# Retention keys and outputs turned in 32x32 blocks by VectorE, and put in place by DMAs, in a Griffin-style encoder block

## The chip, the cores and the metric

The kernel runs on one core of a Trainium2 chip. The metric is device time in microseconds of one execution, the median of several runs; lower is better. A core has a matrix engine (TensorE, PE in the rows, with its weight loads as PEld), VectorE (DVE), ScalarE (ACT), GpSimd (POOL) and SyncE (SP), which here only issues DMAs. Each engine works off its own list of instructions in order. A DMA is issued by an engine's queue and lands later. All matrix inputs and all results are float32.

## The reference, cut to what matters

One layer on 512 tokens of width 2048: a combined projection of the normalised input, a sparse attention (mixer A), a retention (mixer B), two gated merges, an output projection and a gated embedding. The part that the change touches is mixer B, with 8 heads of key and value width 128, and the gate behind it:

```python
rq = rope(rq.reshape(B, L, R_HEADS, R_KEY_DIM), positions)
rk = rope(rk.reshape(B, L, R_HEADS, R_KEY_DIM), positions) * (R_KEY_DIM ** -0.5)
...
scores = jnp.einsum('bnqhd,bnkhd->bnhqk', qc, kc) * intra_decay
intra = jnp.einsum('bnhqk,bnkhe->bnqhe', scores, vc)
kv = jnp.einsum('bnkhd,bnkhe->nbhde', kc * to_end[:, :, None], vc)
...
y = (intra + cross).reshape(B, L, R_HEADS, R_VAL_DIM)
mu = jnp.mean(y, axis=-1, keepdims=True)
var = jnp.mean((y - mu) ** 2, axis=-1, keepdims=True)
y = ((y - mu) * lax.rsqrt(var + EPS)).reshape(B, L, R_WIDTH) * gn_gain
...
b_out = retention_mixer(rq, rk, rv, ret_gn_gain) * jax.nn.silu(rz)
```

The sum over keys for `kv` needs the keys with tokens on the partitions, while the projection gives them with the key's channels on the partitions. The normalised output `y` has tokens on the partitions, and the gate and the next projection want channels there. Both have to be turned once per head.

## The kernel before, in words

The large products are done in float32 accuracy from two-part splits: a weight tile `wraw` (128x1024) is loaded by SP, ScalarE rounds it to `wh` (L156), VectorE subtracts to get `wl` (L161) and, for some tiles, adds two raw tiles in place (L163, tile `wraw`). `gemm_pair` makes two 128-column blocks of the projection together, with seven half-sized products; it issues 112 matmuls (L326) of 512 or 256 columns. Its results leave PSUM through ScalarE copies (`pv`, `e1`, `e2`, `e3`, L265, shown as `pv` and `e`) and VectorE sums (`e_t`, L269), and are added up into the tile `go` (L1094).

The order of the work is written out by hand. `step()` advances a counter, the tick; `gemm_pair` calls it after every second matmul, so that a pair lasts 56 ticks. `later(n, f)` puts `f` off by n ticks. Each engine's instructions stand in the order in which these calls come, and no scheduler changes it: an instruction that waits holds up all that stand behind it on its engine, and a DMA issue that waits holds up SP. Weight loads for coming units (L132) stand on SP between the other DMAs; for some tiles POOL issues an adding DMA on top (L119).

The retention of a head h runs in the shadow of these pairs. For each of the 8 heads there is one pair that projects query and key, and then two pairs for the merge gates. When the key has come out of the first (the second call of `rotate`, its tick is called 0 here), a list `steps` (L993 to L996) sets the rest off:

- tick 3, 5, 7: the rotary sums on VectorE (L904 to L906); tick 9: `queries`, tile `qt` (L913)
- tick 24: `scores` on PE (L920), and `keys(0)`: three PE transposes of 128x128 into the PSUM tile `ps_t` (L931, in `turn`); tick 28: `decay`, tile `at` (L924)
- tick 29: `keys(1)`: ScalarE copies `ps_t` to `kn` with a factor per partition (L939)
- tick 39, 41, 43: `states`: PE makes `ps_kv` from `kn` and the values `rvh` (L945), ScalarE and VectorE chain the states
- tick 51: `values_out` on PE, tile `ps_y` (L960, L962); tick 57: `norm`, with a POOL power (L972); tick 70: `scale`, tile `yn` (L979)
- tick 90: `back(0)`: four PE transposes of `yn` into `ps_t`; tick 94: `back(1)`: ScalarE copies them to `yT` with the group norm's gain (L988), and two ticks later SP stores `yT` to the DRAM tensor `yd` (L989)

So a head has 7 PE transposes, and the 8 heads have 56. After the 8 heads, four pairs make the gate `rz`; in them SP loads `yd` back as `y` (L1127), POOL multiplies it into the gate (L1122) and stores to `bd` (L1123). Much later `b_load` (L1261) loads `bd`, and `split` (L850, L851) makes its two parts for the projection `project_b`.

PSUM has 8 banks that all tiles share; `U` tiles are 69 slots of 128x512 float32.

Of the kernel before, what the change touches and what calls it, by code (L numbers as in the profile page):

```python
# [9 lines left out]
F32 = mybir.dt.float32  # L10
# [4 lines left out]
AF = mybir.ActivationFunctionType  # L15
OP = mybir.AluOpType

L = 512
D = 2048
KT = D // 128  # L20
NH = 8
NT = L // 128
# [13 lines left out]
def block_kernel(tc, xT, pT, posb, posq, w_in, w_v, w_r0, w_r1, w_ik, w_a, w_b, w_o, w_ple, w_gate,  # L36
                 w_gt, w_pt, fgb, tab, gains, cst, dec, out, out_a, out_b):
    nc = tc.nc
    pe, dve, act, pool, sp = nc.tensor, nc.vector, nc.scalar, nc.gpsimd, nc.sync

    with contextlib.ExitStack() as ctx:
# [10 lines left out]
        def U(name, dt=F32):  # L52
            return up.tile([128, L], dt, name=name, tag="u")
# [4 lines left out]
        def P(name):  # L58
            return pp.tile([128, L], F32, name=name, tag="p")
# [4 lines left out]
        def tok(t):  # L64
            return slice(128 * t, 128 * t + 128)
# [114 lines left out]
        def later(n, f):  # L180
            if n <= 0:
                return f()
            tick[1] += 1
            heapq.heappush(soon, (tick[0] + n, tick[1], f))
# [260 lines left out]
        ng, fg, gn = g_sb[:, 0:16], g_sb[:, 16:32], g_sb[:, 32:40]  # L445
# [397 lines left out]
                       for i in range(4 * len(b[1]))])  # L843
            bg.append(lambda run=run: waiting.append(run))

        def split(src, name, lag=0):

            h = U(name + "h", F32R)
            l = U(name + "l", F32R)
            later(lag, lambda: act.activation(h, src, AF.Copy))  # L850
            later(lag and lag + 1, lambda: dve.tensor_sub(l, src, h.bitcast(F32)))  # L851
            return h, l

        def three(o, lhs, rhs, cl, cr):
# [29 lines left out]

        yd, bd, zd, qd, kd = (dp.tile([NH, 128, L], F32, name=n) for n in ("yd", "bd", "zd", "qd", "kd"))
        vd = dp.tile([2, 7, 128, L], F32, name="vd")

        def retention(h):

# [34 lines left out]
                dve.tensor_mul(at.rearrange("p (t q) -> p t q", t=NT), E["ps"].rearrange("p (t q) -> p t q", t=NT),  # L924
                               dect[:, None, 0:128].to_broadcast([128, NT, 128]))

            def turn(src, n):

                ps = P("ps_t")
                for t in range(n):  # L930
                    pe.transpose(ps[:, tok(t)], src[:, tok(t)], ident)  # L931
                return ps[:, 0:128 * n]

            def keys(i):
                if i == 0:
                    E["pk"] = turn(E[1], 3)
                else:
                    E["kn"] = U("kn")
                    act.activation(E["kn"][:, 0:384], E["pk"], AF.Copy, scale=dect[:, 256:257])  # L939

            def states(i):
                if i == 0:
                    ps = E["ps"] = P("ps_kv")
                    for t in range(3):
                        pe.matmul(ps[:, tok(t)], E["kn"][:, tok(t)], rv[:, tok(t)], start=True, stop=True)  # L945
                elif i == 1:
                    E["s"] = U("state")
                    act.activation(E["s"][:, 0:128], E["ps"][:, 0:128], AF.Copy)
                else:
                    for t in (1, 2):  # L950
                        dve.scalar_tensor_tensor(E["s"][:, tok(t)], E["s"][:, tok(t - 1)], g128, E["ps"][:, tok(t)],
                                                 op0=OP.mult, op1=OP.add)

            def values_out(t):
                if t == 0:
                    E["py"] = P("ps_y")
                    E["st"] = S("gst", 24)
                    E["mv"] = S("gmv", 8)
                o = E["py"][:, tok(t)]
                pe.matmul(o, E["at"][:, tok(t)], rv[:, tok(t)], start=True, stop=(t == 0))  # L960
                if t:
                    pe.matmul(o, E["qt"][:, tok(t - 1)], E["s"][:, tok(t - 1)], start=False, stop=True)  # L962
# [19 lines left out]

            def back(i):
                if i == 0:
                    E["pt"] = turn(E["yn"], NT)
                else:
                    E["yT"] = U("yT")
                    act.activation(E["yT"], E["pt"], AF.Copy, scale=gn[:, h:h + 1])  # L988
                    later(2, lambda: sp.dma_start(yd[h], E["yT"]))  # L989

            steps = [(9, queries), (24, scores), (24, lambda: keys(0)), (28, decay), (29, lambda: keys(1))]
            steps += [(n, lambda i=i: states(i)) for i, n in enumerate((39, 41, 43))]
            steps += [(51, lambda t=t: values_out(t)) for t in range(NT)]  # L993
            steps += [(57, norm), (70, scale), (90, lambda: back(0)), (94, lambda: back(1))]
            return rotate

        x_wanted = collections.deque(x_away)
# [119 lines left out]
        for n, u in enumerate(u_rz):  # L1117
            y = B("y2")

            def b_out(i, o, y=y, n=n):  # L1120
                act.activation(o, o, AF.Silu)
                pool.tensor_mul(o, o, y[:, L * i:L * i + L])  # L1122
                pool.dma_start(out=bd[2 * n + i], in_=o)  # L1123

            def y_load(y=y, n=n):
                for i in range(2):
                    sp.dma_start(y[:, L * i:L * i + L], yd[2 * n + i])  # L1127

            later(16 if n else 0, y_load)
            gate_pair(u, b_out)  # L1130
# [128 lines left out]
        def b_load(h):  # L1259
            t = U("bk")  # L1260
            sp.dma_start(t, bd[h])  # L1261
            later(25, lambda: bparts.append(split(t, "b", 1)))

        for n in range(NH // 2):
            if n == NH // 2 - 1:
# [461 lines left out]
```

## Time and profile before

| | |
|---|---|
| median of 3 runs | 1656.47 us (1655.72 to 1656.68) |
| the profiled execution | 1655.59 us |
| its span, first to last instruction | 1653.8 us |
| PE busy | 1645.1 us, 99% of the span |
| DVE, ACT, POOL busy | 79%, 58%, 14% |
| granted TensorE clock, mean | 0.999 of full speed |
| DMA moved | 362.69 MB, 219 GB/s over the span |

The span is the part of the execution that the trace covers; 1.8 us of the profiled execution lie around it. Matmuls are pipelined: a matmul's row shows how long it was under way, and the distance between the starts of two matmuls shows what one costs. In a timeline, equal neighbours are merged into one row with a count.

### The profile page before, as it was taken

How to read it: one execution, taken by the hardware profiler on the slowest of the kernel's cores; microseconds unless marked ns; L12 is line 12 of the kernel's file. 1: busy time of each engine (PE TensorE's matmuls, PEld its weight loads, DVE VectorE, ACT ScalarE, POOL GpSimd, SP SyncE). 2: the span in 40 equal slices, each digit the busy share in tenths (PEclk: the TensorE clock that was granted, in tenths of full speed). 3: DMA queues.
4: the chain of work that ended last, by engine and by line, in shares of the span. 5: the costliest groups of instructions: out<-in, count | busy, mean ns of one | idle time of the engine just before them, and what ended most of it. 6: DMA issues, size and time to landing. Idle time of an engine off the chain costs nothing.

```text
span 1653.8 us, 25255 instructions
## 1 busy us (share of the span) xinstructions
PE 1645.1 (99%) x9334; PEld 1448.0 (88%) x9334; DVE 1305.6 (79%) x2022; ACT 966.2 (58%) x1489; POOL 231.8 (14%) x257
## 2 busy tenths in 40 slices
PE   9999999999999999999999999999999999999998
PEld 8988888888888888888888888888888888888997
DVE  8788879888888888877766766787768877888884
ACT  7556545555555555767776766566644444576653
POOL 2100111111111111112331122100000111100112
PEclk9999999999999999999999999999999999999999
DMA  8327999788788788788988888997565788765973
GB/s 311 117 88 240 326 258 275 192 205 221 187 210 217 188 208 222 188 210 247 255 231 229 213 234 220 247 375 278 178 209 179 189 217 219 211 218 145 247 229 141
DMA packets 129531, 362.69 MB, mean 219 GB/s; under 512 B 15552, under 2 KB 24256, under 8 KB 129408
## 3 DMA queue, kind: packets, MB, share of 16 engines
q1 hardware_dynamic: 89152, 239.77, 41.5%
q0 software_dynamic: 27440, 98.32, 31.7%
q10 hardware_dynamic: 12816, 23.00, 3.8%
q8 instruction: 73, 1.20, 0.3%
q14 instruction: 50, 0.41, 0.1%
HBM read 313.32 MB, written 47.71 MB: 218 GB/s over the span
## 4 chain that ended last, share of the span: by engine, by line
PE 96%; DVE 2%; ACT 1%; issue 0%; DVEq 0%; ACTq 0%
PE ps_p L326 26%; PE ps_v L326 17%; PE ps_q L326 9%; PE ps_r L326 9%; PE ps_w L233 3%; PE ps_w L232 3%; PE ps_w L234 3%; PE ps_vn L874 2%; PE ps_vn L873 2%; PE ps_vn L872 2%; PE ps_iq L232 1%; PE ps_iq L234 1%; PE ps_iq L233 1%; PE ps_pg L233 1%; PE ps_pg L232 1%; PE ps_pg L234 1%
## 5 line engine op out<-in xcount | busy, mean ns | idle before, releaser
L161 DVE TENSOR_TENSOR wl<-wraw,wh 128x1024 fp32r<-128x1024 f32 (+3 forms) x472 | 568.4, 1216 | 157.7 <-ACT wh L156 155.3
L156 ACT ACTIVATE wh<-wraw 128x1024 fp32r<-128x1024 f32 (+3 forms) x471 | 486.8, 1041 | 240.6 <-DVE wraw L163 118.9
L119 POOL DMA_DIRECT2D wraw<-w_in x120 | 106.3, 960 | 574.7 <-DVE wl L161 386.6
L326 PE MATMUL ps_p<-hs,wh 128*128 128x512 f32 x640 | 160.8, 393 | 0.0
L265 ACT ACTIVATE e<-ps_p 128x512 f32<-128x512 f32 x152 | 90.4, 594 | 119.3 <-PE ps_p L326 117.1
L326 PEld LDWEIGHTS ps_p<-hs,wh 128*128 128x128 f32 x640 | 115.0, 189 | 20.5
L326 PE MATMUL ps_p<-hs,wl 128*128 128x256 f32 x640 | 91.8, 284 | 0.0
L326 PEld LDWEIGHTS ps_p<-hs,wl 128*128 128x128 f32 x640 | 83.1, 192 | 0.0
L326 PE MATMUL ps_q<-ha,wh 128*128 128x512 f32 x320 | 80.7, 394 | 0.0
L326 PE MATMUL ps_v<-ha,wh 128*128 128x512 f32 x320 | 80.0, 392 | 0.0
L326 PE MATMUL ps_v<-hs,wh 128*128 128x512 f32 x320 | 79.0, 389 | 0.0
L326 PE MATMUL ps_p<-ha,wh 128*128 128x512 f32 x320 | 79.0, 389 | 0.0
L326 PE MATMUL ps_r<-hs,wh 128*128 128x512 f32 x320 | 79.0, 389 | 0.0
L800 ACT ACTIVATE mk<-relf,thr 128x512 f16<-128x512 f32 (+3 forms) x128 | 66.7, 555 | 16.5 <-DVE go L1094 12.0
L1094 DVE TENSOR_TENSOR go<-e_t 128x256 f32<-128x256 f32 x160 | 68.2, 426 | 5.7
L326 PEld LDWEIGHTS ps_v<-hs,wh 128*128 128x128 f32 x320 | 60.1, 188 | 12.5
L326 PEld LDWEIGHTS ps_p<-ha,wh 128*128 128x128 f32 x320 | 60.1, 188 | 12.5
L326 PEld LDWEIGHTS ps_r<-hs,wh 128*128 128x128 f32 x320 | 60.1, 188 | 12.5
L269 DVE TENSOR_TENSOR e_t<-ps_p,pv 128x512 f32<-128x512 f32 x48 | 33.1, 690 | 47.6 <-ACT e L265 47.5
L326 PEld LDWEIGHTS ps_v<-ha,wh 128*128 128x128 f32 x320 | 59.5, 188 | 12.1
L119 POOL DMA_DIRECT2D wraw<-w_o x24 | 21.1, 938 | 348.6 <-DVE t L356 191.4
L326 PEld LDWEIGHTS ps_q<-ha,wh 128*128 128x128 f32 x320 | 57.5, 189 | 12.1 <-issue 1.7
(481 smaller groups left out, 3812.3 us busy)
## 6 DMA issues: line engine op xcount, KB each, us to landing
wraw<-w_in SPq DMA_DIRECT2D x170, 512.0 KB, 5.1
wraw<-w_in POOLq DMA_DIRECT2D x120, 512.0 KB, 8.3
wraw<-w_o SPq DMA_DIRECT2D x32, 512.0 KB, 4.9
wraw<-w_o POOLq DMA_DIRECT2D x24, 512.0 KB, 6.9
wraw<-w_gate SPq DMA_DIRECT2D x24, 512.0 KB, 5.1
wraw<-w_v SPq DMA_DIRECT2D x16, 512.0 KB, 9.0
wraw<-w_b SPq DMA_DIRECT2D x16, 512.0 KB, 5.8
wraw<-w_a SPq DMA_DIRECT2D x16, 512.0 KB, 3.8
```

What stands on the lines that cost most here:

```text
L119: pool.dma_start(out=view(raw_tiles[r], nk, cols), in_=src[:, k0:k0 + nk, :], accum_op=OP.add)
L156: act.activation(h, raw, AF.Copy)
L161: dve.tensor_sub(l, raw, h.bitcast(F32))
L232: pe.matmul(o, h[:, k, w], a, start=(s == order[0]), stop=False)
L233: pe.matmul(o, h[:, k, w], b, start=False, stop=False)
L234: pe.matmul(o, l[:, k, w], a, start=False, stop=(s == order[-1]))
L265: act.activation(E[n], src, AF.Copy)
L269: f(t, x, y)
L326: pe.matmul(o[:, co], w[:, k], src, start=(n < 4 and begin and k == 0 and j == 0), stop=(ended[n] == 16), skip_group_check=True)
L800: act.activation(bias_e[b][i // per][:, ln * (i % per):ln * (i % per + 1)], relf[:, :ln], AF.Sign, bias=thr[:, q:q + 1])
L872: pe.matmul(o, a[:, tok(t)], h[:, k], start=(s == 0), stop=False)
L1094: dve.tensor_add(o[:, q], c0, c1)
```

## The change

Both turns leave TensorE. VectorE transposes each 32x32 block in place of the 128x128 turn and writes the blocks in an order by which four DMAs, one for each group of 32 partitions, can put them in DRAM as the turned matrix with its columns in a known order of blocks.

For the keys: `keys(0)` at tick 11 is the VectorE transpose into `kb`; `keys(1)` at tick 21 issues four stores from SP to a new DRAM tensor `krd` (32 partitions each, 128 pieces of 384 bytes); `keys(2)` at tick 29 issues one load of `krd` into `kr` (192 KB); `keys(3)` at tick 36 is the ScalarE copy to `kn`, now from `kr`, which puts the blocks in order and applies the factor. `states`, `values_out` and `norm` come two ticks later than before, `scale` stays.

For the outputs: `back(0)` at tick 74 is the VectorE transpose into `yb`; `back(1)` at tick 84 issues four stores to `yd` (128 pieces of 512 bytes each). The copy `yT` is gone. The order of blocks in `yd` is undone by POOL's multiplication, and the gain moves into `split` of the loaded `bd`.

```diff
+        def split(src, name, lag=0, gain=None):
...
+            def low():
+                if gain is None:
+                    dve.tensor_sub(l, src, h.bitcast(F32))
+                else:
+                    dve.scalar_tensor_tensor(l, src, gain, h.bitcast(F32), op0=OP.mult, op1=OP.subtract)
+
+            later(lag, lambda: act.activation(h, src, AF.Copy, scale=1.0 if gain is None else gain))
+            later(lag and lag + 1, low)
...
+        krd = dp.tile([NH, 128, 384], F32, name="krd")
...
-            def turn(src, n):
-                ps = P("ps_t")
-                for t in range(n):
-                    pe.transpose(ps[:, tok(t)], src[:, tok(t)], ident)
-                return ps[:, 0:128 * n]
+            def turn(src, n, name):
+                b = U(name)
+                w = 32 * n
+                dve.transpose(out=b[:, 0:4 * w].rearrange("p (j t c) -> p t j c", j=4, t=n),
+                              in_=src[:, 0:4 * w].rearrange("p (t j c) -> p t j c", t=n, j=4))
+                return b[:, 0:4 * w]
+
+            def send(b, dst):
+                w = b.shape[1] // 4
+                for i in range(4):
+                    sp.dma_start(dst.rearrange("(j r) (i x) -> i r j x", j=4, i=4)[i],
+                                 b[32 * i:32 * i + 32, :].rearrange("r (j x) -> r j x", j=4))
 
             def keys(i):
                 if i == 0:
-                    E["pk"] = turn(E[1], 3)
+                    E["kb"] = turn(E[1], 3, "kb")
+                elif i == 1:
+                    send(E["kb"], krd[h])
+                elif i == 2:
+                    E["kr"] = U("kr")
+                    sp.dma_start(E["kr"][:, 0:384], krd[h])
                 else:
                     E["kn"] = U("kn")
-                    act.activation(E["kn"][:, 0:384], E["pk"], AF.Copy, scale=dect[:, 256:257])
+                    act.activation(E["kn"][:, 0:384].rearrange("p (t i c) -> p i t c", t=3, i=4),
+                                   E["kr"][:, 0:384].rearrange("p (i t c) -> p i t c", i=4, t=3),
+                                   AF.Copy, scale=dect[:, 256:257])
...
             def back(i):
                 if i == 0:
-                    E["pt"] = turn(E["yn"], NT)
+                    E["yb"] = turn(E["yn"], NT, "yb")
                 else:
-                    E["yT"] = U("yT")
-                    act.activation(E["yT"], E["pt"], AF.Copy, scale=gn[:, h:h + 1])
-                    later(2, lambda: sp.dma_start(yd[h], E["yT"]))
-
-            steps = [(9, queries), (24, scores), (24, lambda: keys(0)), (28, decay), (29, lambda: keys(1))]
-            steps += [(n, lambda i=i: states(i)) for i, n in enumerate((39, 41, 43))]
-            steps += [(51, lambda t=t: values_out(t)) for t in range(NT)]
-            steps += [(57, norm), (70, scale), (90, lambda: back(0)), (94, lambda: back(1))]
+                    send(E["yb"], yd[h])
+
+            steps = [(9, queries), (11, lambda: keys(0)), (21, lambda: keys(1)), (29, lambda: keys(2))]
+            steps += [(24, scores), (28, decay), (36, lambda: keys(3))]
+            steps += [(n, lambda i=i: states(i)) for i, n in enumerate((41, 43, 45))]
+            steps += [(53, lambda t=t: values_out(t)) for t in range(NT)]
+            steps += [(59, norm), (70, scale), (74, lambda: back(0)), (84, lambda: back(1))]
...
-                pool.tensor_mul(o, o, y[:, L * i:L * i + L])
+                ov = o.rearrange("p (t i c) -> p t i c", t=4, i=4)
+                v = y[:, L * i:L * i + L].rearrange("p (i t c) -> p t i c", i=4, t=4)
+                pool.tensor_mul(ov, ov, v)
...
-            later(25, lambda: bparts.append(split(t, "b", 1)))
+            later(25, lambda: bparts.append(split(t, "b", 1, gn[:, h:h + 1])))
```

## Rows read from the trace of the kernel before

**Rows 1.** The page: busy time, share of the span and instructions of each engine.

```profile
PE 1645.1 (99%) x9334; PEld 1448.0 (88%) x9334; DVE 1305.6 (79%) x2022; ACT 966.2 (58%) x1489; POOL 231.8 (14%) x257
```

**Rows 2.** Waits of PE, whole span: total us, times, longest.

```profile
PE ps_warm L487 <- DVE warm L464: 1.0, 1, 1.0
```

**Rows 3.** Stretches: us, busy of PE, PEld, DVE, ACT, POOL, clock, DMA share, GB/s.

```profile
256.00:790.00 534.00, 534.00 (x3182) 474.10 (x3181) 448.26 (x691) 309.27 (x407) 90.37 (x96) 1.00 0.81 213
292.30:299.10 6.80, 6.80 (x52) 6.41 (x50) 6.73 (x9) 2.92 (x4) 0.00 (x0) 1.00 0.44 158
```

**Rows 4.** Instructions on tile ps_t: ns min/median/max, first and last start.

```profile
L931 PE MATMUL ps_t<-cs,yn x32: 270/272/273, 318.1 to 754.8; 128*128 128x128 f32 x32
L931 PE MATMUL ps_t<-cs,go x24: 272/273/273, 293.7 to 730.2; 128*128 128x128 f32 x24
```

**Rows 5.** Timeline of PE, head 0: start us, us, instruction, count.

```profile
293.67 0.49 PE L931 MATMUL ps_t<-cs,go 128*128 128x128 f32 x3
293.91 0.95 PE L326 MATMUL ps_q<-ha,wl 128*128 128x256 f32 x6
294.71 1.12 PE L326 MATMUL ps_r<-hs,wl 128*128 128x256 f32 x8
295.66 0.52 PE L326 MATMUL ps_p<-hs,wl 128*128 128x256 f32 x3
...
298.46 0.83 PE L945 MATMUL ps_kv<-rvh,kn 128*128 128x128 f32 x6
299.05 2.10 PE L326 MATMUL ps_v<-ha,wh 128*128 128x512 f32 x8
300.99 1.11 PE L326 MATMUL ps_v<-ha,wl 128*128 128x256 f32 x8
```

**Rows 6.** Timeline of DVE, head 0.

```profile
291.78 0.55 DVE L913 TENSOR_TENSOR qt<-go,dect 128x384 f32<-128x384 f32 x1
292.25 2.35 DVE L161 TENSOR_TENSOR wl<-wraw,wh 128x1024 fp32r<-128x1024 f32 x2
294.64 1.23 DVE L163 TENSOR_TENSOR wraw<-wraw 128x1024 f32<-128x1024 f32 x1
```

**Rows 7.** Timeline of ACT, head 0; in brackets idle time before and what ended it.

```profile
295.98 1.06 ACT L156 ACTIVATE wh<-wraw 128x1024 fp32r<-128x1024 f32 x1 [4.28 <-DVE wraw L163]
```

**Rows 8.** Timeline of SP's queue, head 0, and the landing times of yd<-yT.

```profile
293.49 0.33 SPq L132 DMA_DIRECT2D wraw<-w_in  x1
...
320.33 0.33 SPq L989 DMA_DIRECT2D yd<-yT  x1
320.70 1.46 SPq L132 DMA_DIRECT2D wraw<-w_in  x3
...
DMA to landing us min/median/max: 2.0/2.1/2.2
```

**Rows 9.** Issues by line: KB each, median us to landing.

```profile
y<-yd SPq DMA_DIRECT2D x8, 256.0 KB, 6.2
```

**Rows 10.** Stores in pieces of 128 and 64 bytes (rd<-rvx), and their landing.

```profile
L614 SPq DMA_DIRECT2D rd<-rvx x2: 382/440/499, 73.0 to 73.4; - x2
...
DMA to landing us min/median/max: 1.8/1.8/1.9
```

**Rows 11.** Timelines of DVE and PE, head 6.

```profile
666.94 2.35 DVE L161 TENSOR_TENSOR wl<-wraw,wh 128x1024 fp32r<-128x1024 f32 x2
...
669.62 1.12 PE L326 MATMUL ps_p<-hs,wl 128*128 128x256 f32 x8
...
672.42 0.83 PE L945 MATMUL ps_kv<-rvh,kn 128*128 128x128 f32 x6
```

**Rows 12.** Timelines of DVE and PE, head 3.

```profile
478.11 1.22 DVE L161 TENSOR_TENSOR wl<-wraw,wh 128x1024 fp32r<-128x1024 f32 x1
...
485.44 0.83 PE L945 MATMUL ps_kv<-rvh,kn 128*128 128x128 f32 x6
```

**Rows 13.** Instructions of line L1122, columns as in rows 4.

```profile
L1122 POOL TENSOR_TENSOR go<-go,y x8: 1292/1512/1898, 783.8 to 848.2; 128x512 f32<-128x512 f32 x8
```

More of the change, by code (lines that the diff above doesn't have):

```diff
@@ L844, in block_kernel @@
             bg.append(lambda run=run: waiting.append(run))
-        def split(src, name, lag=0):
+        def split(src, name, lag=0, gain=None):
             h = U(name + "h", F32R)
             l = U(name + "l", F32R)
-            later(lag, lambda: act.activation(h, src, AF.Copy))
-            later(lag and lag + 1, lambda: dve.tensor_sub(l, src, h.bitcast(F32)))
+            def low():
[5 more added lines that the diff above has]
+            later(lag and lag + 1, low)
             return h, l
```

## The prediction

> **What bounds the kernel now.** I read the page first: PE is busy 99% of the span [rows 1]. That alone says little, since a pipelined matmul's row is longer than what the matmul costs, so the waits come second. PE waited once, for 1.0 us, before the first matmul [rows 2]; from then on no semaphore held it up. Third, the retention stage by itself (256 to 790 us): PE is busy all of its 534 us at full clock, VectorE 448 us (84%), ScalarE 309 us (58%), and the DMA engines 81% [rows 3]. So the time there is the sum of what PE issues, every other engine has been early enough so far, and two things decide: how much PE issue the change takes out, and whether any of what it puts in makes PE wait for the first time.
>
> **What is removed.** There are 32 + 24 transposes of 272 ns each [rows 4]; 56 x 0.272 = 15.2 us would be the wrong sum, because a matmul starts before its forerunner has ended. The cost is the distance between starts. From 293.67 to 294.71 PE starts three transposes and six 256-column matmuls; the eight 256-column matmuls after them take 0.95 us to the next start, 0.119 each [rows 5]. So 1.04 - 6 x 0.119 = 0.33 us for three transposes, 0.109 each. The output turn's transposes have the same shape and duration [rows 4], so 56 x 0.109 = 6.1 us. That is all the change can gain: PE does not wait for PSUM banks, so the two banks that a head no longer needs are worth nothing, and neither is the ScalarE copy `yT`.
>
> The Trainium skill (VectorE: DVE Perf Modes, The three transpose paths) gives a 128x128 TensorE transpose as 390 ns in bf16 and VectorE's block transpose as 311 ns. By that figure the estimate would be 56 x 0.39 = 21.8 us; the spacing of the starts says otherwise, and the measurement decides.
>
> **What is added for the keys.** I follow head 0, in the times of the trace of before.
> - VectorE's transpose of 128x384 follows `qt`, of the same size, which took 0.55 us and held the engine 0.47 (291.78 to 292.25) [rows 6]. No row has a transpose; between 0.2 (half of it) and 0.94 (double) I take 0.47, the nearest row's. The result is there at 292.8.
> - SP issues four stores. Two issues in a row start 0.37 apart, and a store of 256 KB landed after 2.0 to 2.2 us [rows 8]. Issues at 292.85 to 293.96, last landing at 296.1. The weight load at tick 23, at 293.49 before [rows 8], now stands behind them, 0.8 us later. Nobody needs its data soon: SP is eight weight tiles ahead of use. Late next would be POOL's adding DMA and the rounding of that tile; if that cover were gone it would be 0.8 us a head.
> - SP then holds the load of `kr` until the stores have landed, to 296.1, and the next weight loads stand behind it by some tenths, under the same cover. No row shows such a load in this place. Below stands the 2.0 us of a store [rows 8], above the 6.2 us of the loads of `yd` [rows 9]. I take 2.4, near the lower end, because the DMA engines are busy 44% in this stretch against 81% in the stage [rows 3], with one weight load in front. `kr` is there at 298.5.
> - ScalarE: the rounding at 295.98 waits for VectorE's addition [rows 6, 7], so it starts 0.47 later, at 296.45; it and the next one keep ScalarE until 298.5. The copy to `kn`, about 0.55 by `qt`'s size, ends at 299.1, 6.85 us after VectorE's hand-over at 292.25.
> - PE: `ps_kv` started at 298.46. Three transposes less bring it 0.33 forward; two ticks more are four 512-column matmuls at 1.94 / 8 = 0.24 each, 0.97 back [rows 5]. PE comes there at 299.1 too: a wait of 0 to 0.1 us. The two ticks by which the state chain and `values_out` move shift demand and supply alike.
>
> Head 6 is the tightest. Its hand-over is at 666.94 and `ps_kv` starts 5.48 us later; in head 0 that is 6.21, in head 3 7.33 [rows 5, 6, 11, 12]. The second `wl` of head 6 ends at 666.94 + 2.35 = 669.29, and PE reads it at 669.62 [rows 11]. With VectorE 0.47 later and PE 0.33 earlier, PE waits 0.5 there, and then `kn` (673.8) is 0.25 later than PE (673.55): 0.75 in all. In head 3 there are 1.1 us to spare. Taking five heads like head 0, two like head 3 and head 6: 5 x 0.1 + 0.75 = 1.3 us given back.
>
> **What is added for the outputs.** `yn` is ready before tick 74, and nothing on PE waits for `yb`: the gate stage reads `yd` for its first heads after the eighth. SP stands at the four stores until VectorE has turned `yn`; before, it stood until ScalarE had made `yT`, and later (the store went at 320.33 [rows 8]). Three issues more are 3 x 0.37 = 1.1 us of SP, hidden by the same lead of the weight loads. VectorE gets 0.61 us more (0.47 x 512/384) in front of the next weight splits. VectorE had 86 of 534 us idle [rows 3] and the change takes 8 x (0.47 + 0.61) = 8.6 of them, so on average there is room. Locally I bound the effect by nothing and 0.5 us a head (head 6's case) and take 0.1: 0.8 us.
>
> **What costs nothing.** POOL's product (1.5 us, eight times [rows 13]) now reads runs of 32; if it took double, 1.5 us would stand before the next adding DMA of POOL, which the lead of the weight loads hides. The split with gain keeps its count of instructions, and the matmuls of the last pairs and of the projection hide it. DRAM traffic grows by 8 x 2 x 192 KB = 3 MB of 363 MB.
>
> **The sum.** 6.1 - 1.3 - 0.8 = 4.0 us. The profiled execution took 1655.59 us, so 1651.6; the median of the runs is 0.9 us above that execution, so **1652.5 us**. A measurement of this kernel tells about 0.2%, 3.3 us, from no change: below 1653.2 is faster, above 1659.8 slower. The forecast's own range is 1650.4 (no wait at all) to 1653.1.
>
> **The rivals.**
>
> *The round trip eats the gain.* If the transpose holds VectorE twice as long (0.94), or `kr` lands half a microsecond later, five heads wait about 0.55 us and head 6 1.2, with 0.8 for the outputs 4.8 us: 1655.2 us, no change that can be told. For it: head 0's margin came out at zero, from a load whose time no row gives. Against: I added each step in series and took the longer of two ScalarE roundings as certain.
>
> *The load of `kr` lands late, and PE waits in every head.* The place is `states` in front of PE, in order, so each delay past the margin goes straight to the end. At the 6.2 us of the loads of `yd` [rows 9] the copy comes 3.8 us later: 5 x 3.85 + 4.55 + 2 x 2.7 = 29 us of waits, +24 net, 1680 us. At 4.3 us it is 14 us, +8.7 net, 1665 us. It decides from a landing of about 3.6 us, where the net loss passes 3.3 us. For it: 81% DMA load in the stage; against: the quiet stretch just here [rows 3], and 192 KB in place of 256.
>
> *The short pieces make the stores slow.* If stores in pieces of 384 bytes landed after twice the 2.1 us, `kn` would come 2.1 us later, with 5 x 2.15 + 2.85 + 2 x 1.0 = 15.6 us of waits: 1666 us. Stores in pieces of 128 and 64 bytes landed after 1.8 to 1.9 us [rows 10], which speaks against it, though at a quiet time. The Trainium skill (DMA: Bandwidth & Descriptors, Specifications) states 512 bytes as the least transfer for full rate and a read-modify-write below it; by that rule this rival would be the outcome, and the 64-byte stores of this trace do not bear it out for single small stores.
>
> *It does not do what it says*, in that PE's issue goes on at the same pace for another reason: transposes that lay in the shadow of weight loads would free nothing. The spacing of the starts [rows 5] shows each taking its own 0.109 us, so I give this almost nothing.
>
> **How the numbers follow.** The forecast 0.50 (faster); the round trip that eats the gain 0.32 (same); late `kr` 0.13 and slow stores 0.05 (slower). The range goes from 1650.0 (the whole 6.1 us, and half a microsecond of scatter) up into the late-`kr` case at 1661.0; what is left out is most of the two slower cases and a little below.
>
> **What would show it.** In the profile of after, the PE rows of `ps_t` are gone and PE has fewer instructions. If the forecast holds, the waits of PE name `ps_kv` for ScalarE's `kn` with some tenths of a microsecond, in few heads, head 6 first. VectorE's transposes show 0.5 to 0.7 us, the stores land after about 2 us, and `kr` after 2.4. A `kr` landing near 4 us and eight PE waits at `ps_kv` of over 1 us each would show the slower case; waits of PE at an L326 matmul for `wl` would show VectorE's room as the mis-sized term. A gain clearly over 6.1 us would mean that the spacing of starts misses a part of what a transpose costs.

## The result, and the profile after

The changed kernel takes 1665.43 us (median of 6 runs, 1662.95 to 1669.14) against 1656.19 us before (6 runs, 1655.72 to 1656.68): ratio 1.006, 95% interval 1.0046 to 1.0074. It is slower by 9.2 us. The prediction said 1652.5, so the sign was wrong, and the time lies above the range. The profiled execution of after took 1665.03 us, 9.44 more than that of before.

The page of after, its span, its lines of busy time and the chain's shares by engine:

```profile
span 1663.2 us, 25259 instructions
...
PE 1643.0 (99%) x9278; PEld 1442.4 (87%) x9278; DVE 1313.7 (79%) x2038; ACT 963.3 (58%) x1481; POOL 233.0 (14%) x257
...
PE 87%; DVE 6%; ACT 3%; DMA 3%; issue 1%; SPq 0%; DVEq 0%; ACTq 0%
```

PE has lost its 56 transposes and still shows 99%, as in [rows 1], because the rows of pipelined matmuls overlap. The busy share would have told nothing; the chain does, since the parts that are not PE have grown to 13%. The waits of PE (engine, tile and line <- what ended it: us in all, times, longest) answer to [rows 2]:

```profile
PE ps_kv L969 <- ACT kn L961: 11.2, 7, 2.6
PE ps_warm L487 <- DVE warm L464: 1.0, 1, 1.0
PE ps_r L326 <- DVE wl L161: 0.2, 1, 0.2
```

In seven of eight heads PE now stands in front of `ps_kv` for the copy `kn`. That copy waits for the load `kr`. The instructions of the new tiles (columns as in [rows 4]; under each queue's line its time from issue to landing):

```profile
L940 DVE STREAM_TRANSPOSE kb<-go x8: 569/572/575, 293.1 to 736.6; 128x384 f32<-128x384 f32 x8
L948 SPq DMA_DIRECT2D krd<-kb x32: 303/423/1032, 293.7 to 738.8; - x32
DMA to landing us min/median/max: 1.6/1.7/2.5
...
L958 SPq DMA_DIRECT2D kr<-krd x8: 338/338/338, 297.6 to 741.4; - x8
L961 ACT ACTIVATE kn<-kr,dect x8: 614/614/617, 300.8 to 744.6; 128x384 f32<-128x384 f32 x8
DMA to landing us min/median/max: 3.0/4.0/5.0
```

The transpose, the stores and the copy are near what was forecast; the load is not: 4.0 us at the median, not 2.4. Head 4 shows the whole round trip. Its chain of waits (start us, us, engine or DMA and what):

```profile
544.83 0.55 DVE qt L921
545.38 0.50 DVE kb L940
...
547.21 1.68 DMA krd<-kb
549.04 4.44 DMA kr<-krd
553.56 0.62 ACT kn L961
554.23 0.94 PE ps_kv L969 x6
```

The DMAs of SP's queue in the same head say why the load is long:

```profile
545.89 1.75 SPq L948 DMA_DIRECT2D krd<-kb  x4
547.74 0.38 SPq L132 DMA_DIRECT2D wraw<-w_in  x1
549.04 0.34 SPq L958 DMA_DIRECT2D kr<-krd  x1
549.47 0.38 SPq L132 DMA_DIRECT2D wraw<-w_in  x1
```

The 512 KB weight load of tick 23 goes out at 547.74, between the stores (tick 21) and the read-back (tick 29). It landed 5.2 us after its issue, at 552.98; `kr`, issued 1.3 us behind it, came in at 553.48, half a microsecond after it. So the small load that PE waits for shared the DMA engines with a large one that nobody awaited.

Where the time went, stretch by stretch, I take from the starts of PE's matmuls. In each trace and head I read the start of the first matmul at or after a tick, counted from the second `rotate`; the lengths between two such starts, after minus before, are summed over the eight heads. The variants of the experiments stand here too (us):

```
ticks of a head          12-26  26-38  38-47  47-58  88-100 100-112 | stage
the changed kernel       -2.57  +0.91 +13.15  +0.16   -3.36   +0.17 | +8.45
kr_first                 -2.58  +2.04  +2.06  +0.16   -3.36   +0.17 | -1.51
kr_from_act              -2.58  +1.61 +26.68  +0.82   -3.36   +0.17 | +23.34
kr_from_act_one_load     -2.57  +0.92 +10.53  +0.16   -3.36   +0.16 | +5.85
keys_only                -2.57  +0.91 +15.54  +0.15   +0.11    0    | +14.13
outputs_only              0      0      0      0      -3.36   +0.17 | -3.19
queries_behind           -1.91  +0.33  +1.57  +0.16   -3.36   +0.16 | -3.05

                         12-26  26-38  38-72         88-100 100-112 | stage
states_later             -2.57  +0.91  +1.2          -3.36   +0.05  | -3.76
first_and_later          -2.57  +1.21  +1.2          -3.36   +0.07  | -3.46
queries_behind_later     -2.57  +0.27  +0.45         -3.36   +0.06  | -5.15
turn_behind_wl           +1.80  +2.03  +8.47         -1.92   +4.20  | +20.02
```

The key transposes lay in ticks 12 to 26 and gave 2.57 us, those of the outputs in 88 to 100 and gave 3.36. The waits for `kn` lie in 38 to 47 and took 13.15: by head 1.66, 2.83, 0.94, 0.31, 1.95, 2.20, 2.47 and 0.80. In the seven heads in which the view of waits names one, it has 0.23 to 0.25 us less than the table (11.2 in all), because it counts idle time only from the end of the last matmul's row. The 0.91 in 26 to 38 I put down to `wl`: 0.60 of them lie in head 6, where the view has its wait for `wl`; the other 0.30, in heads 1 and 3, it does not name on PE. The execution is 9.44 us longer: 8.45 in the stage and 0.84 ahead of it, nearly all in the first 15 us, which no part of the change touches; I take that for scatter (the profiled execution of before lies 0.6 us under its median). After the stage the difference stays as it is.

### The profile page after: what moved, and what is told of

Read it like the earlier page. It is cut to its first block, busy times and chain, and to the rows that moved or that the text cites. A ratio compares the mean times of both kernels' runs of the same rounds, so it can differ in the third digit from the quotient of the medians.

```text
span 1663.2 us, 25259 instructions
## 1 busy us (share of the span) xinstructions
PE 1643.0 (99%) x9278; PEld 1442.4 (87%) x9278; DVE 1313.7 (79%) x2038; ACT 963.3 (58%) x1481; POOL 233.0 (14%) x257
## 4 chain that ended last, share of the span: by engine, by line
PE 87%; DVE 6%; ACT 3%; DMA 3%; issue 1%; SPq 0%; DVEq 0%; ACTq 0%
PE ps_p L326 23%; PE ps_v L326 15%; PE ps_q L326 8%; PE ps_r L326 7%; PE ps_w L233 3%; PE ps_w L232 3%; PE ps_w L234 3%; PE ps_vn L881 2%; PE ps_vn L880 2%; PE ps_vn L879 2%; DMA kr<-krd 2%; PE ps_iq L234 1%; PE ps_iq L232 1%; PE ps_iq L233 1%; DVE wl L161 1%
## 5 line engine op out<-in xcount | busy, mean ns | idle before, releaser
L326 PEld LDWEIGHTS ps_q<-ha,wh 128*128 128x128 f32 x320 | 57.5, 189 | 12.1 <-issue 1.7
```

The source lines that it names most:

```text
L326: pe.matmul(o[:, co], w[:, k], src, start=(n < 4 and begin and k == 0 and j == 0), stop=(ended[n] == 16), skip_group_check=True)
```

## The experiments

Three causes were thinkable for a slow `kr`: that data just stored is slow to read back; that the load stands in SP's queue behind the weight load; that it shares the DMA engines with it, whatever the queue. And the two halves of the change had to be parted.

### The load ahead of the weight load

`kr_first`: the load at tick 22, ahead of the weight load of tick 23.

```diff
-            steps = [(9, queries), (11, lambda: keys(0)), (21, lambda: keys(1)), (29, lambda: keys(2))]
+            steps = [(9, queries), (11, lambda: keys(0)), (21, lambda: keys(1)), (22, lambda: keys(2))]
```

> The load of kr is issued at tick 22, ahead of the weight load of tick 23, which then waits on SP until the stores have landed (issue about 1.5 us later than in the changed kernel). Theories ring and engines: nothing stands in front of the load any more, it lands after 2.0 to 2.4 us, PE waits 0.1 to 0.5 us a head, 1653 to 1655. Theory read-back: it still takes 3 to 5 us, 1662 to 1668. A fourth outcome: PE begins to wait for weights (wl) because SP holds them up longer; then the waits of PE move from ps_kv to L326.

Measured: 1654.58 us (1653.44 to 1655.28, 11 runs), ratio 0.999 (0.9981 to 0.9999) to before. SP's DMAs in head 4, the tile `kr` with its landing, and the waits of PE:

```profile
540.43 1.75 SPq L948 DMA_DIRECT2D krd<-kb  x4
543.55 0.34 SPq L958 DMA_DIRECT2D kr<-krd  x1
543.99 0.85 SPq L132 DMA_DIRECT2D wraw<-w_in  x2
```

```profile
L958 SPq DMA_DIRECT2D kr<-krd x8: 338/338/338, 296.5 to 730.4; - x8
...
DMA to landing us min/median/max: 2.3/2.4/2.8
```

```profile
PE ps_kv L969 <- ACT kn L961: 0.9, 2, 0.5
PE ps_r L326 <- DVE wl L161: 0.8, 1, 0.8
```

With the load in front of both weight loads, which go out 0.4 and 0.9 to 1.9 us behind it, it lands after 2.4 us, the very figure of the forecast, and 10.85 us come back (1665.43 to 1654.58). The bytes and their path through DRAM are the same, so reading back just stored data is not slow in itself. The weight loads go out later, and that costs something: the losses in ticks 26 to 38 rise from 0.91 to 2.04, now mostly in heads 5 and 6. What is left in 38 to 47, 2.06 us, is the margin that the round trip lacks even with a fast load.

### The load from another queue

`kr_from_act`: ScalarE issues the load, three ticks earlier.

```diff
-                    sp.dma_start(E["kr"][:, 0:384], krd[h])
+                    act.dma_start(E["kr"][:, 0:384], krd[h])
...
-            steps = [(9, queries), (11, lambda: keys(0)), (21, lambda: keys(1)), (29, lambda: keys(2))]
+            steps = [(9, queries), (11, lambda: keys(0)), (21, lambda: keys(1)), (26, lambda: keys(2))]
```

> The load of kr is issued from ScalarE's queue (tick 26) in place of SP's (tick 29). Theory ring: in the changed kernel the load landed 3.0 to 5.0 us after its issue because it stood behind the 512 KB weight load in SP's own ring; from the other queue it lands after about 2.1 to 2.4 us, kn is ready near 6.9 us after VectorE's hand-over, PE waits 0.1 to 0.5 us a head, and the time is 1653 to 1655. Theory engines: the ring does not matter, the 16 DMA engines themselves are taken by the weight load; it still lands after 3 to 5 us and the time stays 1662 to 1668. Theory read-back: data just written to DRAM comes back slowly in itself: the same 1662 to 1668.

Measured: 1678.32 us (1675.21 to 1684.5, 4 runs), ratio 1.0138 (1.012 to 1.0156). That is outside every range of the expectation. The load has ScalarE's queue to itself and is slower still:

```profile
L958 ACTq DMA_DIRECT2D kr<-krd x8: 326/326/328, 296.9 to 753.6; - x8
...
DMA to landing us min/median/max: 3.7/5.3/5.9
```

SP's DMAs in head 0 show what it shares the DMA engines with:

```profile
293.07 1.93 SPq L948 DMA_DIRECT2D krd<-kb  x4
295.11 1.81 SPq L132 DMA_DIRECT2D wraw<-w_in  x2
```

In heads 0 and 4 two weight loads, 1 MB, have been issued when `kr` starts; in heads 1, 2, 5, 6 and 7 the second goes out 0.2 to 0.5 us behind `kr`. In the changed kernel it goes out 0.4 us behind `kr` too (1.9 in head 3), but there it stands behind `kr` in the same queue. Head 3, where the second comes only 1.9 us behind `kr` here as well, lands after 3.7 us, the other seven after 4.9 to 5.9. So to stand behind a weight load in SP's own queue is not the main cause: another queue is no better. Whether it is the second weight load that makes 5.3 us of 4.0, the next one tries.

### The same, with one weight load beside it

`kr_from_act_one_load`: a store holds SP.

```diff
+        held = dp.tile([NH, 128, 16], F32, name="held")
...
-                    sp.dma_start(E["kr"][:, 0:384], krd[h])
+                    act.dma_start(E["kr"][:, 0:384], krd[h])
...
+            steps = [(9, queries), (11, lambda: keys(0)), (21, lambda: keys(1)), (26, lambda: keys(2))]
+            steps += [(24, scores), (28, decay), (36, lambda: keys(3)),
+                      (29, lambda: sp.dma_start(held[h], E["kr"][:, 0:16]))]
```

The load is issued at tick 26 by ScalarE, as above; a small store of a part of `kr` makes SP stand from tick 29 until `kr` has landed, so that only the weight load of tick 23 is beside it.

> As kr_from_act, but SP stands still behind the weight load of tick 23 until kr has landed (a store of 16 columns of kr to a scratch tensor, which adds 8 KB a head and is not part of the computation), so that one weight load and not two is under way beside the load of kr. Theory engines: kr lands 3 to 5 us after its issue as in the changed kernel, from whichever queue; 1661 to 1670. Theory ring: it lands after 2.4 us, as in kr_first, and the 5.3 us of kr_from_act came from the second weight load; 1653 to 1656.

Measured: 1662.53 us (1661.72 to 1665.09, 5 runs), ratio 1.0044 (1.003 to 1.0058). The load and PE's wait for what comes of it:

```profile
L959 ACTq DMA_DIRECT2D kr<-krd x8: 326/326/327, 296.6 to 735.7; - x8
...
DMA to landing us min/median/max: 3.3/3.4/5.2
```

```profile
PE ps_kv L970 <- ACT kn L962: 8.6, 7, 2.1
```

So the landing goes by the weight loads that `kr` meets: 2.4 us with none in front, 3.4 beside one, 5.3 where a second runs beside it from the other queue. Shared DMA engines account for it, whichever queue issues. The changed kernel's own 4.0 lies 0.6 above the 3.4, and the landing times of the two traces say where from. In all eight heads of the changed kernel `kr` comes in 0.5 to 0.6 us after the weight load that was issued ahead of it in the same queue; here, from the other queue, it comes in 0.4 to 0.5 us after it in seven heads (1.8 in the last). What differs is that weight load: it took 4.7 us at the median there, with the next one issued behind `kr`, and 4.2 here, with none. The kernel of before shows 3.5 to 3.6. Why the load in front is slower in the changed kernel was not tried by a run of its own.

### The two halves

`keys_only`: keys by VectorE, and outputs on PE as before, with the multiplication, the gain and `split` of before:

```diff
-                    E["yb"] = turn(E["yn"], NT, "yb")
+                    E["pt"] = P("ps_t")
+                    for t in range(NT):
+                        pe.transpose(E["pt"][:, tok(t)], E["yn"][:, tok(t)], ident)
                 else:
-                    send(E["yb"], yd[h])
+                    E["yT"] = U("yT")
+                    act.activation(E["yT"], E["pt"], AF.Copy, scale=gn[:, h:h + 1])
+                    later(2, lambda: sp.dma_start(yd[h], E["yT"]))
...
-            steps += [(59, norm), (70, scale), (74, lambda: back(0)), (84, lambda: back(1))]
+            steps += [(59, norm), (70, scale), (90, lambda: back(0)), (94, lambda: back(1))]
```

> Only the keys go through VectorE and DRAM, with the changed kernel's ticks; the outputs are turned on PE as before. If the two halves are independent, the time is the changed kernel's plus the output half's gain: 1665.4 + 3.1 = 1668.5, range 1665 to 1672, with PE's waits for kn of 1 to 3 us a head. Rival: the output half has a share in the loss (its stores and SP's issues delay the next head's loads): 1665 or less.

`outputs_only`: outputs by VectorE, and keys on PE at the ticks of before:

```diff
             def keys(i):
                 if i == 0:
-                    E["kb"] = turn(E[1], 3, "kb")
...
+                    E["pk"] = turn_pe(E[1], 3)
                 else:
                     E["kn"] = U("kn")
...
+                    act.activation(E["kn"][:, 0:384], E["pk"], AF.Copy, scale=dect[:, 256:257])
...
+            steps = [(9, queries), (24, scores), (24, lambda: keys(0)), (28, decay), (29, lambda: keys(1))]
+            steps += [(n, lambda i=i: states(i)) for i, n in enumerate((39, 41, 43))]
+            steps += [(51, lambda t=t: values_out(t)) for t in range(NT)]
+            steps += [(57, norm), (70, scale), (74, lambda: back(0)), (84, lambda: back(1))]
```

> The keys are turned on PE as before; only the outputs are turned by VectorE and stored in place. By the starts of the two traces the output half gains 0.42 us a head, so 1656.2 - 3.4 = 1652.8, range 1652.3 to 1653.3, with no wait of PE in the stage. Rival: VectorE's 0.61 us in front of the weight splits or SP's three more issues cost PE something: 1653.5 to 1656.

Measured: keys alone 1671.06 us (1670.63 to 1674.18, 4 runs), ratio 1.0095 (1.008 to 1.0111); outputs alone 1653.11 us (1652.31 to 1653.75, 11 runs), ratio 0.9981 (0.9972 to 0.999). With the keys alone PE waits seven times for `kn`, 12.1 us in all, the longest 2.4. In ticks 38 to 47 this run loses 2.4 us more than the whole change (15.54 and 13.15), 1.6 of them in head 5 by the granted clock, as the last section shows. With the outputs alone this is all that PE waits for:

```profile
PE ps_warm L487 <- DVE warm L464: 1.0, 1, 1.0
```

The output half is what the forecast took the whole change for: the transposes leave (-3.36) and hardly anything comes back (+0.17, the rest of the forecast's 0.8 did not turn up). The whole loss is in the key half. The difference lies in the time that the result has: `yd` is read in another stage, `kn` is wanted some 7 us later.

### More time for the keys

`states_later`: the states, and all that hangs on them, eight ticks later:

```diff
-            steps += [(24, scores), (28, decay), (36, lambda: keys(3))]
-            steps += [(n, lambda i=i: states(i)) for i, n in enumerate((41, 43, 45))]
-            steps += [(53, lambda t=t: values_out(t)) for t in range(NT)]
-            steps += [(59, norm), (70, scale), (74, lambda: back(0)), (84, lambda: back(1))]
+            steps += [(24, scores), (28, decay), (44, lambda: keys(3))]
+            steps += [(n, lambda i=i: states(i)) for i, n in enumerate((49, 51, 53))]
+            steps += [(61, lambda t=t: values_out(t)) for t in range(NT)]
+            steps += [(67, norm), (78, scale), (82, lambda: back(0)), (92, lambda: back(1))]
```

> The copy to kn, the states, values_out, norm, scale and the output turn all come 8 ticks later (about 2.8 us of PE); the transfers stay as in the changed kernel. If the whole loss is PE's wait for kn, PE no longer waits at ps_kv (or under 0.3 us in one or two heads), the gain of the 56 transposes shows in full, 1656.2 - 2.6 - 3.4 = 1650.2, range 1649.5 to 1651.5, and the scatter between runs shrinks to that of the kernel before. Rival: the wait turns up elsewhere (slots held longer, the states late for values_out), 1654 or more.

Measured: 1653.55 us (1652.40 to 1655.31, 11 runs), ratio 0.9985 (0.9976 to 0.9994). The load lands as late as ever, after 2.8, 3.8 and 4.8 us (least, median, most), but PE's waits are nearly gone:

```profile
PE ps_p L326 <- DVE wl L161: 0.3, 1, 0.3
PE ps_kv L969 <- ACT kn L961: 0.2, 1, 0.2
PE ps_r L326 <- DVE wl L161: 0.2, 1, 0.2
```

So a late load costs nothing as such; it costs by what PE's next instruction lacks of margin. The expected time was missed by some 3 us. By the starts 2.1 us are still lost in the stage (0.91 and 1.2 in the table): about 0.5 of them for `kn` in head 6, and the rest around matmuls that need `wl`, where the view of PE's waits names only a part. The median lies 1.1 us over the profiled execution, which no trace explains.

`first_and_later`: both cures together:

```diff
-            steps = [(9, queries), (11, lambda: keys(0)), (21, lambda: keys(1)), (29, lambda: keys(2))]
+            steps = [(9, queries), (11, lambda: keys(0)), (21, lambda: keys(1)), (22, lambda: keys(2))]
...
-            steps += [(24, scores), (28, decay), (36, lambda: keys(3))]
+            steps += [(24, scores), (28, decay), (44, lambda: keys(3))]
```

(and the four later steps as above)

> Both mends together: the load of kr ahead of the weight load (tick 22), and kn, states, values_out, norm, scale and the output turn 8 ticks later. With kr landing after 2.4 us PE has about 2.5 us to spare at ps_kv, so no wait there. What is left by the theory is PE's wait for wl behind VectorE's transpose (0.9 to 2.0 us in the runs so far): 1656.2 - 6.0 + 1.5 = 1651.7, range 1650.8 to 1652.6. Rival: the weight load of tick 23, held up by some 3 us, is missed later, and PE or ScalarE waits for its data: 1653 or more.

Measured: 1653.03 us (1652.42 to 1654.96, 11 runs), ratio 0.9981 (0.9972 to 0.999). That is above the expected range (1650.8 to 1652.6). The cures don't add up, since each takes away the same wait; what remains is in the same heads and of the same size as in `states_later`, most of it around matmuls that need `wl`. Whether that is the price of VectorE's transpose ahead of the weight splits, the next ones try.

### VectorE's transpose elsewhere

`turn_behind_wl`: first behind the splits that it delayed, at tick 17 in place of 11, with the load at tick 22 and the states twelve ticks later:

```diff
-            steps = [(9, queries), (11, lambda: keys(0)), (21, lambda: keys(1)), (29, lambda: keys(2))]
+            steps = [(9, queries), (17, lambda: keys(0)), (21, lambda: keys(1)), (22, lambda: keys(2))]
```

> As first_and_later, and VectorE's transpose of the keys comes at tick 17, behind the two weight splits and the addition that it stood in front of; the load of kr stays ahead of the weight load, kn at tick 48 and all behind it 12 ticks later than in the changed kernel. If the waits for wl come from the transpose's place, they are gone: 1656.2 - 6.0 = 1650.2, range 1649.6 to 1651.0. Rival: SP now holds the weight load for some 6 us, or kn is late again by about 1 us a head: 1652 or more.

Measured: 1674.22 us (1672.44 to 1676.42, 4 runs), ratio 1.0109 (1.0095 to 1.0123). The issues of the stage, KB each and median us to landing, and the waits of PE:

```profile
wraw<-w_in SPq DMA_DIRECT2D x99, 512.0 KB, 6.4
...
wraw<-w_in POOLq DMA_DIRECT2D x75, 512.0 KB, 10.9
```

```profile
PE ps_p L326 <- DVE wl L161: 7.3, 12, 1.2
PE ps_v L326 <- DVE wl L161: 2.9, 3, 1.2
```

This is the rival of that expectation. The stores stand at SP until VectorE has turned the block, 3.5 us later (4.9 in head 3), and behind them stand the weight loads. The first of them went out 7.7 to 9.0 us after VectorE was done with `qt`, where it went out after 1.2 in the kernel before, the next ones half a microsecond apart behind it, and they landed in a bunch: the median weight load of SP took 6.4 us against 5.0 in the same stretch of before, POOL's adding loads 10.9 against 8.6. Now PE waits for weights (the two longest groups are shown above; three heads also wait for `kn`, 2.4 us), and the stage is 20.0 us longer than before. The lead of the weight loads, on which the forecast counted, hides the delays of the changed kernel but not these.

`queries_behind`: then in the place of `qt`, which nobody awaits so early: the transpose at tick 9, `queries` at tick 33, the load at tick 22:

```diff
-            steps = [(9, queries), (11, lambda: keys(0)), (21, lambda: keys(1)), (29, lambda: keys(2))]
-            steps += [(24, scores), (28, decay), (36, lambda: keys(3))]
+            steps = [(9, lambda: keys(0)), (21, lambda: keys(1)), (22, lambda: keys(2))]
+            steps += [(24, scores), (28, decay), (33, queries), (36, lambda: keys(3))]
```

> The load of kr ahead of the weight load (tick 22), states and all behind them at the changed kernel's ticks, and VectorE's transpose takes the place of qt (tick 9), while qt, which nothing reads before values_out, goes behind the weight splits (tick 33). VectorE is then no later at the splits than before. If the waits for wl (0.9 to 2.4 us in the runs so far) come from the 0.55 us that the transpose adds in front of the splits, they fall to under 0.5 us, and kn is ready 0.47 us earlier, so PE waits at ps_kv for under 0.5 us in all: 1656.2 - 6.0 + 0.5 = 1650.7, range 1650.0 to 1651.7. Rival: the wl waits come from PE being earlier, not VectorE later; then they stay at 1.5 us or more and the time is 1652 or more.

`queries_behind_later`: the same with the states and all behind them eight ticks later, as in `states_later`:

> As queries_behind, with kn, states, values_out, norm, scale and the output turn 8 ticks later. If any of queries_behind's loss is PE's wait for kn, this one is faster by that much, 1650.2 (1649.6 to 1651.2); if not, the two are within 0.5 us of each other.

Measured: 1652.83 us (1651.82 to 1653.78, 11 runs), ratio 0.998 (0.9971 to 0.9989), and 1651.81 us (1651.32 to 1652.58, 7 runs), ratio 0.9973 (0.9962 to 0.9984). What PE waits for in the second, beside the wait before the first matmul that all have:

```profile
PE ps_kv L969 <- ACT kn L961: 0.2, 1, 0.2
```

Both times lie above the expected ranges (1650.0 to 1651.7, and 1649.6 to 1651.2), but not for the reason that the rival gave: PE has no wait for `wl` left in either view. The first still loses 1.57 us for `kn` in ticks 38 to 47, and 0.7 in head 5 at a wait for ScalarE's `wh`, which the second does not have and no run explains. With VectorE's new work in the place of work that can wait, the weight splits are no later than before, and in the second 5.15 us of the 5.93 stay in the stage. This version beats both kernels, the one before by 4.5 us (1656.28 beside it to 1651.81). Beside the outputs alone (0.9972 to 0.999) the intervals overlap: the key half is worth some 1.3 us (1653.11 to 1651.81, medians on two chips), which these runs don't make certain.

## Why the prediction was wrong

**The gain was right.** 2.57 + 3.36 = 5.93 us against 6.1, or 0.32 and 0.42 a head against 0.33 and 0.44. The distance between starts was the right price; the durations of the rows would have said 15.2.

**VectorE and the stores were right.** The transpose holds VectorE for 0.50 us (0.47 taken); the four issues take 1.75 to 2.4 us (1.44 taken); the last of the stores landed 3.6 to 4.4 us after the hand-over (3.85 taken). Each piece-wise store landed after 1.7 us, less than the 2.1 of the store of 256 KB, so the rival of the slow stores falls. The Trainium skill (DMA: Bandwidth & Descriptors, Specifications) speaks for it with its least transfer of 512 bytes for full rate; the pieces of 384 bytes here do not bear it out, at 48 KB a store. The stores of `yb`, in pieces of 512 bytes and 64 KB each, landed after 1.7 us at the median too.

**The step that failed is "I take 2.4" for the landing of `kr`.** It measured 3.0 to 5.0 us, 4.0 at the median. Since SP issued the load up to a microsecond later too, in three heads, `kr` was there 7.2 to 8.7 us after the hand-over and not 6.25, and `kn` 7.9 to 9.4 and not 6.85. In head 0 and its like the margin was zero to begin with, so each tenth went to the end of the kernel: 13.15 us where the forecast had 0.75 (five times 0.1, and 0.25 in head 6). The heads differ in part as forecast: head 3 with its 1.1 us to spare loses least, 0.31, and head 6 loses 2.47; but head 1, which the forecast had like head 0, loses most, 2.83, because its landing was the slowest, 5.0 us.

The bounds were right (2.0 and 6.2) and the choice between them was not. I chose by the stretch's mean: DMA engines busy 44% [rows 3]. A mean says how much room there is in seven microseconds, not what is in flight at the moment of issue, and the order of the issues was there to be read: tick 21 the stores, tick 23 a weight load of 512 KB, tick 29 the load of `kr`. The text even says "with one weight load in front", and gives it no price. That load was in the trace of before as well [rows 8]; there it landed after 3.5 to 3.6 us. A row for a load beside or behind such a transfer was missing. The runs show what stood in its place: `kr` came in half a microsecond behind the weight load in front of it, so its time goes by that load. They give 2.4 us with none in front, 3.4 to 4.0 with one, and 5.3 where a second ran beside it from another queue. The Trainium skill (DMA: Bandwidth & Descriptors, Issuing engines are not separate DMA queues) says that DMAs of all issuing engines run on the same 16 engines and interleave; `kr_from_act` agrees with its 5.3 us.

**The rival of the late load came true**, place and price: at a landing of 4.3 us it gave 14 us of waits and 1665 us; measured were 4.0, 13.15 and 1665.4. It had 0.13. The point from which it decides lies a little lower than the 3.6 us given: `kr_from_act_one_load`, at 3.4, is already 0.4% slower than before; at 2.3 to 2.4 none is but `turn_behind_wl`, which waits for weights.

**The wait for `wl` in head 6 was right.** 0.60 us against 0.5; VectorE's place ahead of the splits was the second thing that `queries_behind_later` had to mend.

**The small terms.** The outputs cost 0.17 us in the stage, not 0.8. The copy `kn` takes 0.614 us, not 0.55. POOL's product with its runs of 32 takes 1.52 us at the median, where it took 1.51 [rows 13].

## What to carry to other kernels

A turn through DRAM puts a store and a load in series, here 1.7 us at the median and 2.4 at best behind the issues; price the load by when the large load ahead of it lands (here half a microsecond before it), which the order of the issues tells and a mean share does not. Put the small load that somebody awaits ahead of the large one that nobody does (moving it to another queue did not help here, and let a second large one run beside it), give its reader more ticks, and put new work of an engine in the place of work that can wait. Where the result has a stage's time, as the outputs here, the same turn cost 0.17 us in eight heads.

## What was not expected of the hardware

A stand-still of PE can cost more than itself, because the granted clock can fall in it or just behind it. In head 0 of `kr_from_act` PE waited 3.45 us for `kn`. PE's timeline around it:

```profile
298.50 1.20 PE L326 MATMUL ps_v<-ha,wh 128*128 128x512 f32 x4
...
303.15 1.65 PE L969 MATMUL ps_kv<-rvh,kn 128*128 128x128 f32 x6 [3.45 <-ACT kn L961]
304.45 2.05 PE L326 MATMUL ps_v<-ha,wh 128*128 128x512 f32 x4
```

and the stretches ahead of, during and after it (us, then busy us and instructions of PE, PEld, DVE, ACT and POOL, granted clock, DMA share, GB/s):

```profile
295.00:302.00 7.00, 4.71 (x27) 3.51 (x25) 6.62 (x10) 2.01 (x2) 0.00 (x0) 1.00 0.83 228
302.35:309.10 6.75, 5.95 (x24) 5.56 (x25) 2.52 (x5) 4.66 (x6) 0.87 (x1) 0.50 0.51 120
309.20:316.00 6.80, 6.80 (x40) 5.93 (x39) 3.56 (x7) 2.22 (x4) 1.79 (x2) 1.00 0.91 166
```

The granted clock stood at 0.50, 1.2 of 2.4 GHz, for 6.75 us, from late in the wait on; four 512-column matmuls took 2.05 us where they had taken 1.20. From the first matmul on `ps_kv` to tick 58 PE took 11.10 us in this head and 8.40 in the five heads of the run without such a stretch, so the clock cost 2.7 us on top of the wait of 3.45. The same is in heads 1 and 4 of that run (from 370.57 and 565.13, 3.4 us each), where it cost 1.4 and 1.5 us, and once in `keys_only` (from 621.26), where it cost 1.6. PE's 19.6 us of waits for `kn` in `kr_from_act`, 0.24 us more at each of the seven as in the changed kernel, and these 5.6 us make 26.9; by the starts ticks 38 to 58 lost 27.5.

The length of the wait alone does not decide: in `keys_only` the clock fell at a wait of 1.9 us and stayed up at one of 2.4. The profiled execution of the changed kernel, whose longest wait is 2.6 us, shows no such stretch. The spread of its runs, 1662.95 to 1669.14, was not traced; the two slowest, 1669.14 and 1669.01, have a mean granted clock of 0.997, the other four 0.998 or 0.999.
